# Decoder layer on one core: quadrant sums of the weights added by GpSimd in two parts of 512 columns instead of by VectorE

## The chip, the cores and the metric

The kernel runs on one core of a Trainium2 chip. The metric is the device time of one execution in microseconds, the median of several runs. The engines are called by their names in the profile: PE (TensorE, the matrix engine; PEld is its weight load), DVE (VectorE), ACT (ScalarE), POOL (GpSimd) and SP (SyncE, which here only issues DMAs). Each engine runs its own instructions in the order in which they were put down, and semaphores hold an instruction until what it reads is there.

## The reference

One decoder layer on 512 tokens of width 2048: a normed and modulated input h, a wide projection, two branches (sliding-window attention, and a gated delta rule in 32 heads of 128), a gated merge and an output projection. Cut to what matters here:

```python
proj = h @ w_in
...
o = gated_delta_rule(dq, dk, dv, g, beta)
o = rms_norm(o, dn_norm_w) * jax.nn.silu(dz)
y_b = o.reshape(B, T, DN_VAL) @ w_o_dn
y = jax.nn.sigmoid(mg_a) * y_a + jax.nn.sigmoid(mg_b) * y_b
return x + gate * (y @ w_out)
```

The change concerns w_o_dn and w_out, the weights of two of these products, before they are used.

## The kernel before, in words

All products are made in float32 out of three matmuls on split operands: a weight tile `raw` is split into `whi` (ScalarE, L61) and `wlo` (VectorE, L62), and L255 to L257 multiply `whi` with both parts of the input and `wlo` with the high part. `channel_tile` (L266) makes one 128x512 tile of the projection with 16 such triples and calls `pump` after every second one. `pump` (L90) lets all other work of the stage go a step further: weight loads and splits that are due, generators with a delay counted in pumps (`go`), and generators with a budget per pump (`paced`, L81): such a generator yields a cost, and goes on when the budgets of enough pumps have summed up to it.

In the stage `delta_heads` (L639) sixteen pairs of heads are worked through, g = 0 to 15, with five channel tiles each (query, two values, two gates; L791). Beside the tiles of one pair run the steps of the pair before:

- `queries` (L821): SyncE loads the decay rows `E` of both heads (L726) and kT (L829); GpSimd masks `E` in place (affine select, L731); ScalarE turns it into exponentials (L737, four per head); GpSimd multiplies the loaded rows `qe` (L848) with the query (L869); a few small products `py`, `pu` follow on PE (L881 to L888), with a copy `Y` (L883).
- `scan` (L902): four chunks of the recurrence, with PE, ScalarE and VectorE in turn. Then the root chain on VectorE: `ms` (L964), a reciprocal square root in ten short operations of 128x8 (L68, and three times L71 to L73), and the scaling of the output `osb` (L971, twice). PE transposes `osb` into `pto` (L296), and VectorE multiplies it by the gate (L978).
- Values go through a convolution on VectorE (`yv`, L593 three times, L600) and are transposed by PE (`ptv`) and copied by ScalarE (`vt`, L818).
- In the first part of the stage VectorE also works off a triangular solve (L766, L774, at the end L784).

The later products with w_o_dn and w_out follow Strassen's scheme with seven products of half-size matrices (`PRODUCTS`, L34). Four of the seven weight factors are sums of weight quadrants. `weight_sums` (L1170) makes them while the heads run: it is started at g = 4 (L658) with a budget of 1.75 per pump, and for each of 24 sets it loads four quadrant pieces of 128x1024 into the tiles q00, q10, q11 and q01 (L1182, one buffer each, 512 KB), yields 10, and then four times adds two pieces in place (L1186), yields 4, stores the sum to DRAM (L1188, `g_d` or `f_d`) and yields 2. The next set's loads go into the same four tiles, so each waits until the store of the old sum has landed. All these DMAs stand in SyncE's one queue, with the loads of raw weights, `qe`, `E`, `kT` and the rest.

`behind` (L259) gives an instruction a dependency without a semaphore on the last matmul issued: it sets where the instruction is put into its engine's order, and holds nothing when the program runs. The order within each engine comes from a scheduler that places instructions by priorities and estimated durations; so another engine or duration can change the places of others.

Of the kernel before, what the change touches and what calls it, by code (L numbers as in the profile page):

```python
# [11 lines left out]
ALU = mybir.AluOpType  # L12
# [5 lines left out]
T = 512  # L18
# [27 lines left out]
class Layer:  # L46
# [1123 lines left out]
    def weight_sums(self, wk):  # L1170

        nc, a = self.nc, self.a
        sets = [(a["w_od"][0], self.g_d[0]), (a["w_od"][1], self.g_d[1]), (a["w_out"], self.f_d)]
        for w, dst in sets:
            for n in range(2):
                for i in range(2):
                    for h in range(2):
                        cols = slice(h * 1024, (h + 1) * 1024)
                        q = []
                        for c, r in ((0, 0), (1, 0), (1, 1), (0, 1)):  # L1180
                            t = wk.tile([P, 1024], F32, tag=f"q{c}{r}", name=f"q{c}{r}", bufs=1)
                            nc.sync.dma_start(out=t, in_=w[2 * c + n, 2 * r + i][:, cols])  # L1182
                            q.append(t)
                        yield 10.0
                        for f, (x, y) in enumerate(((0, 1), (1, 2), (0, 2), (2, 3))):
                            self.behind(nc.vector.tensor_tensor(out=q[f], in0=q[x], in1=q[y], op=ALU.add))  # L1186
                            yield 4.0
                            self.behind(nc.sync.dma_start(out=dst[n, f, i][:, cols], in_=q[f]))  # L1188
                            yield 2.0

# [508 lines left out]
```

## Time and profile before

| | us |
|---|---|
| runs | 2904.66, 2897.58, 2900.23 |
| median | 2900.23 |
| profiled execution, its own time | 2904.38 |
| its span, first to last instruction | 2902.6 |
| busy PE / DVE / ACT / POOL | 2831.1 / 1964.7 / 1187.8 / 138.7 |
| first and last addition L1186 (start) | 1347.9 / 2135.3 |

All times in the traces are microseconds from the span's start. A matmul's busy time overlaps that of the next, so PE's idle time, not its busy time, tells what is lost. In a row of groups, "x96 | 118.6, 1235 | 0.1" reads: 96 instructions, 118.6 us busy in total, 1235 ns mean, 0.1 us of idle time of the engine just ahead of them. In a row of waits stand who waited, for whom, the total in us, how often and the longest. In a row of one line's instructions stand the shortest, median and longest in ns.

### The profile page before, as it was taken

What the parts mean: (1) busy time and instruction counts of PE and PEld (TensorE: products, weight loads), DVE (VectorE), ACT (ScalarE), POOL (GpSimd) and SP (SyncE); (2) the same over time, 40 slices, a digit from 0 to 9 for tenths busy, and PEclk for the clock granted to TensorE, in tenths of its full rate; (3) what the DMA queues carried; (4) which work ended last, traced back from release to release, by engine and by line L of the source; (5) the groups of instructions that cost most, each with busy time, mean ns of one, the idle gap of its engine ahead of it and who ended that gap; (6) DMA issues with size and microseconds to landing.
All of it is one profiled execution on the core that took longest, in us unless ns stands there. A gap on an engine that the chain in (4) does not pass through costs nothing.

```text
span 2902.6 us, 38619 instructions
## 1 busy us (share of the span) xinstructions
PE 2831.1 (98%) x14396; PEld 2322.2 (80%) x14396; DVE 1964.7 (68%) x3173; ACT 1187.8 (41%) x2381; POOL 138.7 (5%) x124
## 2 busy tenths in 40 slices
PE   6899999999999999999999999999999999999999
PEld 5588888877787888888888888878888788878887
DVE  5776686878768766777766666666656766764666
ACT  3356453334454343433433333333334444433343
POOL 0001000000001000010100000000000000000000
PEclk8999999999999999999999999999999999999999
DMA  9877774322243243434787777777746887885784
GB/s 331 325 237 228 242 249 153 112 92 83 96 140 99 95 153 130 134 117 165 253 262 244 232 251 248 241 227 248 246 149 219 283 301 266 294 276 176 244 319 165
DMA packets 229790, 604.28 MB, mean 208 GB/s; under 512 B 78145, under 2 KB 104257, under 8 KB 189153
## 3 DMA queue, kind: packets, MB, share of 16 engines
q1 hardware_dynamic: 229602, 601.81, 62.2%
q8 instruction: 113, 1.85, 0.3%
q14 instruction: 75, 0.61, 0.1%
HBM read 481.32 MB, written 118.18 MB: 207 GB/s over the span
## 4 chain that ended last, share of the span: by engine, by line
PE 85%; DVE 6%; DMA 6%; ACT 2%; issue 1%; POOL 0%; SPq 0%; DVEq 0%; POOLq 0%; ACTq 0%
PE mm L255 20%; PE mm L257 19%; PE mm L256 19%; PE m L256 5%; PE m L255 5%; PE m L257 5%; DMA E<-g_rows 1%; DVE wlo L62 1%; DVE wa L430 1%; PE S L1377 1%; PE O L1428 1%; PE pv L922 1%; PE po L941 1%; DMA g_d<-q 1%; PE pP L296 1%
## 5 line engine op out<-in xcount | busy, mean ns | idle before, releaser
L255 PE MATMUL mm<-hh,whi 128*128 128x512 f32 x2784 | 1131.7, 407 | 2.8 <-ACT mth L285 2.8
L257 PE MATMUL mm<-hh,wlo 128*128 128x512 f32 x2784 | 1091.0, 392 | 0.0
L256 PE MATMUL mm<-hl,whi 128*128 128x512 f32 x2784 | 1088.7, 391 | 0.0
L62 DVE TENSOR_TENSOR wlo<-raw,whi 128x1024 fp32r<-128x1024 f32 (+1 forms) x532 | 655.1, 1232 | 468.3 <-ACT whi L61 456.1
L61 ACT CAST whi<-raw 128x1024 fp32r<-128x1024 f32 (+1 forms) x532 | 555.3, 1045 | 875.1 <-PE mm L256 630.3
L255 PEld LDWEIGHTS mm<-hh,whi 128*128 128x128 f32 x2784 | 524.7, 188 | 114.1 <-issue 9.2
L257 PEld LDWEIGHTS mm<-hh,wlo 128*128 128x128 f32 x2784 | 523.6, 188 | 114.0 <-issue 0.5
L256 PEld LDWEIGHTS mm<-hl,whi 128*128 128x128 f32 x2784 | 525.0, 189 | 100.5 <-issue 1.4
L737 ACT ACTIVATE E<-E,neg_g 128x128 f32<-128x128 f32 x256 | 81.9, 392 | 109.4 <-POOL E L731 106.0
L1186 DVE TENSOR_TENSOR q<-q,q 128x1024 f32<-128x1024 f32 x96 | 118.6, 1235 | 0.1
L774 DVE TENSOR_TENSOR A<-A,atmp 128x62 f32<-128x62 f32 (+30 forms) x124 | 108.3, 873 | 0.5
L766 DVE TENSOR_TENSOR atmp<-A 128x62 f32<-128x62 f32 (+30 forms) x124 | 107.7, 868 | 0.5
L869 POOL TENSOR_TENSOR qe<-qe,yq 128x512 f32<-128x512 f32 x32 | 51.0, 1611 | 939.1 <-DMA qe<-eg_rows 693.5
L942 ACT COPY osb<-po 128x256 f32<-128x256 f32 x64 | 23.8, 372 | 153.0 <-PE po L941 153.0
L731 POOL TENSOR_SCALAR_AFFINE_SELECT E<-E 128x512 f32<-128x512 f32 x64 | 55.0, 869 | 459.9 <-DMA E<-g_rows 381.6
L924 ACT COPY vn<-pv 128x256 f32<-128x256 f32 x64 | 23.8, 372 | 120.7 <-PE pv L922 120.7
L1401 ACT ACTIVATE sm<-sm,mx,rs 128x256 f32<-128x256 f32 (+1 forms) x128 | 71.7, 562 | 3.5 <-DVE mx L1396 3.5
L593 DVE SCALAR_TENSOR_TENSOR yv<-mm,convh,yv 128x511 f32<-128x511 f32 (+2 forms) x96 | 71.3, 743 | 1.0
L929 DVE TENSOR_SCALAR vs<-vn,kd 128x128 f32<-128x128 f32 x96 | 23.1, 284 | 57.6 <-ACT vn L924 57.6
L430 DVE SCALAR_TENSOR_TENSOR wa<-wa,silu_cb 128x2048 f32<-128x2048 f32 x24 | 54.8, 2284 | 6.4 <-DMA silu_cb<-silu_d 6.4
L915 DVE SCALAR_TENSOR_TENSOR r<-pp,neg_eg,vt 128x128 f32<-128x128 f32 x96 | 29.1, 345 | 40.6 <-PE pp L912 40.5
L941 PE MATMUL po<-vn,E 128*128 128x128 f32 x256 | 46.8, 275 | 0.0
(425 smaller groups left out, 3666.1 us busy)
## 6 DMA issues: line engine op xcount, KB each, us to landing
raw<-in_w_ch SPq DMA_DIRECT2D x158, 1024.0 KB
wa<-in_w_ada_ss SPq DMA_DIRECT2D x32, 1024.0 KB
q<-in_w_od SPq DMA_DIRECT2D x64, 512.0 KB
g_d<-q SPq DMA_DIRECT2D x64, 512.0 KB
raw<-g_d SPq DMA_DIRECT2D x32, 1024.0 KB
raw<-in_w_od SPq DMA_DIRECT2D x24, 1024.0 KB
gw<-in_w_ada_gate SPq DMA_DIRECT2D x16, 1024.0 KB
E<-g_rows SPq DMA_DIRECT2D x64, 256.0 KB
```

The costliest lines, as they stand in the source:

```text
L61: self.nc.scalar.copy(out=hi, in_=src)
L62: self.nc.vector.tensor_tensor(out=lo, in0=src, in1=hi.bitcast(F32), op=ALU.subtract)
L255: nc.tensor.matmul(ps, lhsT=wh, rhs=xh, start=first, stop=False)
L256: nc.tensor.matmul(ps, lhsT=wh, rhs=xl, start=False, stop=False)
L257: self.last_mm = nc.tensor.matmul(ps, lhsT=wl, rhs=xh, start=False, stop=last)
L430: nc.vector.scalar_tensor_tensor(out=wa, in0=wa, scalar=1.0, in1=scb, op0=ALU.mult, op1=ALU.mult, accum_out=t[:, j : j + 1])
L737: self.nc.scalar.activation(E[:, c, :], E[:, c, :], AF.Exp, bias=self.neg_g[:, c, h : h + 1])
L766: eng.tensor_tensor(out=t, in0=A[:, m : m + 1, m + 1 :].to_broadcast([P, m, n]), in1=A[:, :m, m : m + 1].to_broadcast([P, m, n]), op=ALU.mult,
L774: self.behind(eng.tensor_tensor(out=A[:, :m, m + 1 :], in0=A[:, :m, m + 1 :], in1=t, op=ALU.add))
L941: nc.tensor.matmul(po[:, e, :], lhsT=M[e][:, c, :], rhs=vn[:, e, :], start=c == 0, stop=True)
L1186: self.behind(nc.vector.tensor_tensor(out=q[f], in0=q[x], in1=q[y], op=ALU.add))
L1401: nc.scalar.activation(t, t, AF.Exp, scale=r[:, h : h + 1], bias=mx[:, h : h + 1], accum_out=den[:, h : h + 1])
```

## The change

Each addition of two 128x1024 pieces goes from VectorE to GpSimd, and is cut into two additions of 512 columns. The yield of 4 behind an addition becomes a yield of 2 behind each half, so that the sum per set is the same, 34. Loads, stores and tiles are as before. From here on the lines behind L1185 have a number one higher: the addition is L1187 in the changed kernel.

```diff
                         yield 10.0
                         for f, (x, y) in enumerate(((0, 1), (1, 2), (0, 2), (2, 3))):
-                            self.behind(nc.vector.tensor_tensor(out=q[f], in0=q[x], in1=q[y], op=ALU.add))
-                            yield 4.0
+                            for k in (slice(0, T), slice(T, 1024)):
+                                self.behind(nc.gpsimd.tensor_tensor(out=q[f][:, k], in0=q[x][:, k], in1=q[y][:, k], op=ALU.add))
+                                yield 2.0
                             self.behind(nc.sync.dma_start(out=dst[n, f, i][:, cols], in_=q[f]))
                             yield 2.0
```

What moves in the engines' orders, at two places. First VectorE, at the root chain of the head pair whose L971 runs at 1924 us in the trace; `q` are the quadrant pieces, `ms`, `roy` and `rot` the root's small tiles, `osb` the output of the scan. Before:

```order
L72 TENSOR_TENSOR rot<-rot,ms 128x8
L1186 TENSOR_TENSOR q_16333<-q_16333,q_16335 128x1024
L73 SCALAR_TENSOR_TENSOR roy<-rot,roy 128x8
L62 TENSOR_TENSOR wlo<-raw,whi 128x1024
L71 SCALAR_TENSOR_TENSOR rot<-roy 128x8
L836 TENSOR_SCALAR epsq<-ss 128x4
L593 SCALAR_TENSOR_TENSOR yv<-mm,convh,yv 128x511
L72 TENSOR_TENSOR rot<-rot,ms 128x8
L593 SCALAR_TENSOR_TENSOR yv<-mm,convh,yv 128x510
L73 SCALAR_TENSOR_TENSOR roy<-rot,roy 128x8
L593 SCALAR_TENSOR_TENSOR yv<-mm,convh,yv 128x509
```

and now, from the last L72 of the same chain through the scaling L971 and a little beyond:

```order
L72 TENSOR_TENSOR rot<-rot,ms 128x8
L73 SCALAR_TENSOR_TENSOR roy<-rot,roy 128x8
L62 TENSOR_TENSOR wlo<-raw,whi 128x1024
L971 TENSOR_TENSOR osb<-osb,roy 128x512 x2
L836 TENSOR_SCALAR epsq<-ss 128x4
L593 SCALAR_TENSOR_TENSOR yv<-mm,convh,yv 128x511
L593 SCALAR_TENSOR_TENSOR yv<-mm,convh,yv 128x510
L593 SCALAR_TENSOR_TENSOR yv<-mm,convh,yv 128x509
L978 TENSOR_TENSOR zh<-pto,zh 128x512
```

Before, the addition and the three convolution steps stood inside the chain; now they stand behind it. Of the twelve root chains between 1347 and 2140 us, three have this stretched form before (one addition and three L593 inside), and none now. On PE four of the transposes' groups `pto` stand one or two triples of matmuls earlier; nothing else is moved by more than one weight split on ScalarE or VectorE.

Second GpSimd, at the same head pair, with the semaphores that each instruction waits for; `qe` are the rows that are multiplied with the query, `E` the decay rows that are masked; DMAHW are semaphores of DMAs, Pool that of GpSimd itself. Before:

```order
L869 TENSOR_TENSOR qe<-qe,yq 128x512 [waits DVE_49,DMAHW3_49,PE_49,Pool_49]
L869 TENSOR_TENSOR qe<-qe,yq 128x512 [waits DMAHW4_49,PE_49,Pool_49]
L731 AFFINE_SELECT E<-E 128x512 [waits DMAHW5_49,Activation_49]
L731 AFFINE_SELECT E<-E 128x512 [waits DMAHW6_49,PE_49,Activation_49]
L869 TENSOR_TENSOR qe<-qe,yq 128x512 [waits DVE_49,DMAHW1_49,PE_49,Pool_49]
```

and now:

```order
L1187 TENSOR_TENSOR q_16401<-q_16401,q_16403 128x512 [waits DMAHW6_49,DMAHW1_49,DMAHW0_49]
L869 TENSOR_TENSOR qe<-qe,yq 128x512 [waits DMAHW3_49,DVE_49,PE_49]
L869 TENSOR_TENSOR qe<-qe,yq 128x512 [waits DMAHW4_49,PE_49]
L1187 TENSOR_TENSOR q_16401<-q_16401,q_16403 128x512
L731 AFFINE_SELECT E<-E 128x512 [waits DMAHW5_49,Activation_49]
L731 AFFINE_SELECT E<-E 128x512 [waits DMAHW6_49,PE_49,Activation_49]
L1187 TENSOR_TENSOR q_16403<-q_16403,q_16405 128x512 [waits DMAHW7_49,Pool_49]
L1187 TENSOR_TENSOR q_16403<-q_16403,q_16405 128x512 [waits Pool_49]
L1187 TENSOR_TENSOR q_16405<-q_16401,q_16405 128x512 [waits DMAHW2_49,Pool_49]
```

One half addition is now in front of the multiplications, one between them and the masks, and the other six of the set behind (three are shown). Over the eleven head pairs with masks behind them, ten half additions stand between L869 and both masks, and two more between the first and the second mask. In the last head pair the two multiplications and the last halves are mixed. The half additions wait for the DMAs that load their pieces (and store the sums before) and for GpSimd's own earlier halves; none of them waits for PE, ACT or DVE.

## The prediction

> **What bounds the kernel now.** I read the page first, then its chain, then the stage of the changed line by windows, then who waits there.
>
> ```profile
> span 2902.6 us, 38619 instructions
> PE 2831.1 (98%) x14396; PEld 2322.2 (80%) x14396; DVE 1964.7 (68%) x3173; ACT 1187.8 (41%) x2381; POOL 138.7 (5%) x124
> PE 85%; DVE 6%; DMA 6%; ACT 2%; issue 1%; POOL 0%; SPq 0%; DVEq 0%; POOLq 0%; ACTq 0%
> L1186 DVE TENSOR_TENSOR q<-q,q x96: 1207/1218/1665, 1347.9 to 2135.3; 128x1024 f32<-128x1024 f32 x96
> ```
>
> TensorE is busy 98% of the span and makes 85% of the chain; DVE, which loses work, is 6% of it. The 96 additions lie between 1347.9 and 2135.3 us. So the first question is what TensorE still loses there (columns: stretch, length, busy time of PE, PEld, DVE, ACT, POOL, granted clock, DMA share, GB/s):
>
> ```profile
> 1340.00:1500.00 160.00, 155.19 (x803) 129.13 (x802) 114.95 (x190) 65.48 (x143) 14.16 (x8) 0.98 0.73 238
> 1500.00:1700.00 200.00, 197.71 (x1051) 164.85 (x1050) 123.07 (x209) 76.52 (x180) 12.96 (x12) 1.00 0.75 247
> 1700.00:1900.00 200.00, 197.42 (x1044) 164.28 (x1043) 126.42 (x210) 76.12 (x183) 16.43 (x12) 1.00 0.75 246
> 1900.00:2140.00 240.00, 235.72 (x1233) 196.30 (x1232) 156.64 (x255) 91.14 (x217) 15.28 (x14) 0.99 0.72 235
> 1452.10:1458.90 6.80, 4.95 (x25) 4.06 (x26) 3.21 (x5) 3.08 (x7) 0.64 (x1) 0.50 1.11 322
> 1926.50:1930.00 3.50, 3.50 (x12) 2.81 (x11) 2.98 (x5) 1.75 (x4) 0.00 (x0) 0.51 0.41 158
> ```
>
> Of 800 us TensorE is idle 4.81 + 2.29 + 2.58 + 4.28 = 14.0 us. Two of its waits are followed by stretches at half clock; with 4.95 and 3.50 us of work in them these cost 2.5 + 1.7 = 4.2 us. So 18.2 us, 0.6% of the time, is all that a perfect cover of this stage could return. What TensorE waits for (waited, times, longest):
>
> ```profile
> PE pto L296 <- DVE osb L971: 5.1, 3, 2.8
> PE py L881 <- DMA raw<-in_w_ch: 3.9, 1, 3.9
> PE ptv L296 <- DVE yv L600: 1.8, 1, 1.8
> PE ptv L296 <- DVE zh L978: 1.7, 1, 1.7
> PE py L881 <- ACT vt L818: 1.3, 2, 0.7
> ACT E L737 <- POOL E L731: 69.7, 14, 9.3
> SPq L1188 <- DVE q L1186: 74.6, 37, 8.1
> ```
>
> The last two are other engines: ScalarE waits 69.7 us for GpSimd's masks, and SyncE 74.6 us for the additions whose stores it issues.
>
> **The change part by part.** It takes 96 x 1235 ns = 118.6 us off DVE and puts 192 half additions on GpSimd. The nearest row is the one GpSimd operation of two SBUF tiles of 128x512 in this stage; the masks, which share its queue, are below it:
>
> ```profile
> L1186 DVE TENSOR_TENSOR q<-q,q 128x1024 f32<-128x1024 f32 x96 | 118.6, 1235 | 0.1
> L869 POOL TENSOR_TENSOR qe<-qe,yq x32: 1260/1506/2380, 1093.4 to 2127.5; 128x512 f32<-128x512 f32 x32
> L731 POOL TENSOR_SCALAR_AFFINE_SELECT E<-E x64: 624/635/4532, 186.4 to 2062.8; 128x512 f32<-128x512 f32 x64
> ```
>
> At the median, 192 x 1.506 = 289 us in 787 us (242 at the shortest, 457 at the longest): GpSimd stays under 60% and bounds nothing by its sum. By order the adds carry waits for loads and for GpSimd itself, none for TensorE, so they run when their loads have landed and not at DVE's place.
>
> *The root chain on DVE: gain.* Where an addition stood inside the chain L964 to L971 (the first pair of rows under the change), DVE's chain was stretched, with three L593 also inside. That is so in three heads of the stage, and "pto <- L971" is waited for exactly 3 times.
>
> ```profile
> 1919.12 0.16 DVE L71 SCALAR_TENSOR_TENSOR rot<-roy 128x8 f32<-128x8 f32 x1
> 1921.50 1.02 DVE L71 SCALAR_TENSOR_TENSOR rot<-roy 128x8 f32<-128x8 f32 x1
> 1922.55 1.18 DVE L72 TENSOR_TENSOR rot<-rot,ms 128x8 f32<-128x8 f32 x1
> 1924.35 1.68 DVE L971 TENSOR_TENSOR osb<-osb,roy 128x512 f32<-128x512 f32 x2
> 1921.21 2.51 POOL L869 TENSOR_TENSOR qe<-qe,yq 128x512 f32<-128x512 f32 x2 [63.37 <-DMA qe<-eg_rows]
> 1923.67 1.22 POOL L731 TENSOR_SCALAR_AFFINE_SELECT E<-E 128x512 f32<-128x512 f32 x2
> ```
>
> This is the largest of the three: the stretched chain ran into GpSimd's two multiplications. Now all chains have the short form, and would end before those. I take the whole row and the half clock behind it: -(5.1 + 1.7) = -6.8 us. By order TensorE also takes four of its pto groups one or two triples of matmuls earlier, which spends part of what the shorter chain gives; and if GpSimd's adds meet the chain none of it comes. The term lies between -6.8 and 0; the rows of the orders decide for the first. Next late is then ptv, whose 1.8 and 1.7 us hang on DVE operations that come after ScalarE's tanh.
>
> *Port contention: small loss.* In those rows a 128x8 operation of 0.16 us took 1.18 beside a GpSimd operation: 1.02 us of holding per GpSimd operation. All 192 adds could hold DVE 196 us, none could hold it 0. DVE without the additions is busy (521.1 - 118.6) / 800 = 50%, so half of them, 98 us, is a fair upper value, less than the 118.6 removed. DVE's load therefore falls, but a held operation is late by 1 us where the addition before it made it late by 1.2. I take +1.5 us on TensorE, between 0 and the third rival below. The Trainium skill (SBUF — State Buffer, Who interferes with whom) says that a DVE instruction with two SBUF inputs and a GpSimd instruction that reads SBUF exclude each other, and that the second is blocked until the first is done. By it the hold would be the whole add, 289 us for 192 and not 196; the trace agrees on who is held, and its holds are about 1.0 of 1.26 us.
>
> *The masks behind the adds: loss.* GpSimd's queue now has adds between the multiplications L869 and the masks L731 (the second pair there). Over the eleven heads with masks, 10 stand ahead of both masks and 2 ahead of the second alone: 12 x 1.506 = 18.1 us (15.1 to 28.6) more of ScalarE's wait for masks, if their inputs are there. Behind that wait ScalarE holds weight casts, PSUM copies and the tanh of TensorE's next work:
>
> ```profile
> 1446.07 4.53 POOL L731 TENSOR_SCALAR_AFFINE_SELECT E<-E 128x512 f32<-128x512 f32 x1 [1.44 <-DMA E<-g_rows]
> 1445.70 4.41 DVE L784 TENSOR_TENSOR A<-A,bet 128x4096 f32<-128x4096 f32 x1
> 1450.64 1.28 ACT L737 ACTIVATE E<-E,neg_g 128x128 f32<-128x128 f32 x4 [9.25 <-POOL E L731]
> ```
>
> Here a DVE operation held the mask, ScalarE stood 9.25 us, and TensorE's longest wait (py, 3.9 us) followed; so short waits are covered and long ones are not. On the average 8.9 us of TensorE's idle (14.0 - 5.1) stand against 69.7 us of this wait, 13%; at the margin it can be all. I take 40%, between them but nearer to the average, since the mean wait is 69.7 / 14 = 5.0 us and the covered ones are of that size: +7.2 us. The adds themselves wait for the loads of their quadrants, and a late load would hold the qe and the masks queued behind; SyncE issues most of those loads ahead of E's, so I cost this at nothing beyond the 28.6. Against this, the removed additions no longer hold the masks: two masks took 3.20 us in one head where the median makes 1.27.
>
> ```profile
> 1722.08 3.20 POOL L731 TENSOR_SCALAR_AFFINE_SELECT E<-E 128x512 f32<-128x512 f32 x2
> 1723.13 1.65 DVE L1186 TENSOR_TENSOR q<-q,q 128x1024 f32<-128x1024 f32 x1
> ```
>
> About 1 of those 1.9 us is the addition's; I take three such heads, at the same 40%: -1.2 us.
>
> *SyncE: small gain.* The store of a sum is ahead of loads of qe and E, which the masks need. One such link is on the chain in order of time:
>
> ```profile
> 1569.62 1.23 DVE q L1186
> 1570.87 7.39 DMA g_d<-q
> 1579.65 5.56 DMA E<-g_rows
> 1587.16 2.15 ACT E L737 x7
> ```
>
> With adds that run as soon as loads land, SyncE's 74.6 us mostly go; it then waits for the landing of the store or for TensorE instead. Were GpSimd late, each store would be later by up to one add. Between -4 and +4; I take -1.0 us.
>
> Sum: -6.8 + 1.5 + 7.2 - 1.2 - 1.0 = -0.3 us, from 2904.4 (span 2902.6 and 1.8 around it) to 2904.1. The profiled execution lies 4.2 us above the median of 2900.2; on the median the forecast is 2900 us: no change that shows (0.3%, 8.7 us, is about what this kernel's measurement can tell).
>
> **The rivals.** *DVE's relief wins.* The chain's waits go, SyncE runs ahead, masks come earlier, and TensorE keeps 14 of the 18.2 us: 2886 us. For it: the three irregular chains and the three waits match, and 521 us of DVE fall to 402. Against it: 8.9 us of the idle hang on ScalarE and loads.
>
> *The masks come later and ScalarE stops TensorE (slower).* All 18.1 us of the adds reach TensorE, with half clock behind two more waits (4.2 us): 2900 + 18.1 + 4.2 - 6.8 = 2916 us. It decides once an add between L869 and L731 meets a head whose ScalarE wait is already above about 5 us. For it: the 9.25 us case. Against it: that one was 4.5 us from a single operation.
>
> *A run of adds meets the root chain.* GpSimd runs eight adds back to back, and each short operation of the chain loses 1.02 us: 8.2 us in each of 12 heads, 98 us: 2998 us. The skill's rule would give this too. Against it: by order the runs stand after the masks, and the chain ahead of L869; only the last head's qe has adds around it.
>
> That the change does nothing because DVE is off the path is the forecast's own neighbour, 2900 us.
>
> **How the numbers follow.** No change that shows 0.46; DVE's relief 0.29; masks 0.22; runs of adds 0.03. The faster and the no-change case lie side by side, so the range covers both: it goes from the relief's 2886 to just under the masks' 2916, 2914; the runs and the outer parts of both cases are the 2 in 10 left out. Faster 0.29, same 0.46, slower 0.25.
>
> **What would show it.** Right: GpSimd some 430 us busy and DVE near 1.85 ms; "pto <- L971" gone from TensorE's waits; ScalarE's wait for L731 up by 10 to 18 us; TensorE's idle of the stage 10 to 18 us. Wrong: L71 to L73 at 1 us in many heads with pto waiting behind them; or ScalarE's wait for masks smaller than before; or adds far from 1.5 us.

## The result, and the profile after

The changed kernel takes 2933.6 us (median of 4 runs, 2927.4 to 2936.3) against 2900.2 us before: 1.0114 times, 95% interval 1.0102 to 1.0127. It is 33.4 us slower, where 2900 us was forecast. The profiled execution took 2927.35 us.

From the page of the changed kernel, the span, the busy times and the chain:

```profile
span 2925.6 us, 38733 instructions
PE 2836.7 (97%) x14396; PEld 2324.9 (79%) x14396; DVE 1913.6 (65%) x3077; ACT 1186.8 (41%) x2381; POOL 422.8 (14%) x316
PE 82%; DMA 7%; DVE 6%; ACT 2%; issue 1%; SPq 1%; POOL 1%; DVEq 0%; POOLq 0%; ACTq 0%
```

GpSimd is as busy as forecast. VectorE is not: without its additions it should stand at 1964.7 - 118.6 = 1846.1 us, and it stands at 1913.6. The operations left on it took 67.5 us longer. The stage by windows (columns as in the prediction):

```profile
1340.00:1500.00 160.00, 148.30 (x748) 122.36 (x746) 100.38 (x157) 61.97 (x132) 55.44 (x37) 0.96 0.71 228
1500.00:1700.00 200.00, 194.12 (x1021) 161.23 (x1022) 106.73 (x184) 74.69 (x177) 75.73 (x58) 0.99 0.74 240
1700.00:1900.00 200.00, 195.29 (x1033) 161.83 (x1032) 110.86 (x185) 74.41 (x181) 85.53 (x61) 1.00 0.72 235
1900.00:2140.00 240.00, 232.98 (x1210) 193.51 (x1209) 131.94 (x209) 89.73 (x210) 96.83 (x69) 0.99 0.74 237
```

TensorE is idle 11.7 + 5.9 + 4.7 + 7.0 = 29.3 us here, against 14.0 before. What TensorE waits for in the stage (here 1340 to 2200 us), and the two waits of ScalarE and SyncE that the prediction named:

```profile
PE pd L937 <- DVE vs L929: 13.8, 5, 5.4
PE ptv L296 <- DVE zh L978: 9.3, 6, 3.4
PE py L881 <- DMA g_d<-q: 3.2, 2, 1.9
PE py L881 <- ACT vt L818: 2.9, 1, 2.9
ACT E L737 <- POOL E L731: 68.3, 12, 8.6
SPq L1189 <- POOL q L1187: 59.6, 23, 7.7
```

"pto <- L971" is gone, as forecast. ScalarE's wait for masks is where it was (69.7 before). New is pd, which waits for the scaling of `vn` by `kd` into `vs` (L929), and ptv's wait for L978 has grown from 1.7 to 9.3 us. Two more waits, 1.6 us of ptv for L600 and 2.4 us of pu, lie ahead of 1340 us, since the additions now begin at 1305 us. L929 before the change (shortest/median/longest in ns):

```profile
L929 DVE TENSOR_SCALAR vs<-vn,kd x96: 278/284/290, 1127.5 to 2177.1; 128x128 f32<-128x128 f32 x96
```

and after it, with GpSimd's additions, the root's L73 and the convolution steps:

```profile
L929 DVE TENSOR_SCALAR vs<-vn,kd x96: 272/284/1331, 1125.0 to 2205.5; 128x128 f32<-128x128 f32 x96
L1187 POOL TENSOR_TENSOR q<-q,q x192: 1254/1292/2346, 1305.2 to 2164.8; 128x512 f32<-128x512 f32 x192
L73 DVE SCALAR_TENSOR_TENSOR roy<-rot,roy x36: 166/166/170, 1371.4 to 2154.1; 128x8 f32<-128x8 f32 x36
L593 DVE SCALAR_TENSOR_TENSOR yv<-mm,convh,yv x96: 729/743/751, 1098.1 to 2170.5; 128x511 f32<-128x511 f32 x32, 128x510 f32<-128x510 f32 x32, 128x509 f32<-128x509 f32 x32
```

L929, never above 290 ns before, reaches 1331. The root's L73 isn't held at all, nor is L593, which takes one of its two tiles from PSUM. Two places of the timeline show holds at work (start, length, engine, what; x is a count, in brackets the wait ahead). First GpSimd, VectorE and TensorE around 1420 us:

```profile
1417.59 10.12 POOL L1187 TENSOR_TENSOR q<-q,q 128x512 f32<-128x512 f32 x7
1419.42 1.80 DVE L62 TENSOR_TENSOR wlo<-raw,whi 128x1024 fp32r<-128x1024 f32 x1 [1.64 <-ACT whi L61]
1421.14 1.77 DVE L807 SCALAR_TENSOR_TENSOR zh<-zth,zh 128x512 f32<-128x512 f32 x1
1422.84 2.50 DVE L929 TENSOR_SCALAR vs<-vn,kd 128x128 f32<-128x128 f32 x2
1425.40 1.13 PE L937 MATMUL pd<-vs,k 128*128 128x256 f32 x2 [2.32 <-DVE vs L929]
```

Seven additions run back to back. L62 takes 1.80 us where its median is 1.23, L807 1.77 where it is 0.69, two L929 2.50 where they are 0.57: 0.6 + 1.1 + 1.9 = 3.6 us, of which pd waits 2.3. I read it as turns: an addition, a VectorE operation, the next addition, so that each of these operations is longer by up to most of an addition. Then ptv, around 1953 us:

```profile
1950.38 9.88 POOL L1187 TENSOR_TENSOR q<-q,q 128x512 f32<-128x512 f32 x6
1952.99 2.25 DVE L62 TENSOR_TENSOR wlo<-raw,whi 128x1024 fp32r<-128x1024 f32 x1 [4.79 <-ACT whi L61]
1955.16 1.75 DVE L600 SCALAR_TENSOR_TENSOR yv<-th,yv 128x512 f32<-128x512 f32 x1
1956.83 0.68 DVE L978 TENSOR_TENSOR zh<-pto,zh 128x512 f32<-128x512 f32 x1
1957.56 0.74 PE L296 MATMUL ptv<-ident,yv 128*128 128x128 f32 x4 [3.40 <-DVE zh L978]
```

L978 has a tile in PSUM and isn't held itself, but it stands behind two operations that are, late by 1.0 and 1.1 us.

### The profile page after: what moved, and what is told of

Same layout as the page of the kernel before. It is cut to its first block, busy times and chain, and to the rows that moved or that the text cites. A ratio compares the mean times of both kernels' runs of the same rounds, so it can differ in the third digit from the quotient of the medians.

```text
span 2925.6 us, 38733 instructions
## 1 busy us (share of the span) xinstructions
PE 2836.7 (97%) x14396; PEld 2324.9 (79%) x14396; DVE 1913.6 (65%) x3077; ACT 1186.8 (41%) x2381; POOL 422.8 (14%) x316
## 4 chain that ended last, share of the span: by engine, by line
PE 82%; DMA 7%; DVE 6%; ACT 2%; issue 1%; SPq 1%; POOL 1%; DVEq 0%; POOLq 0%; ACTq 0%
PE mm L255 19%; PE mm L256 18%; PE mm L257 18%; PE m L256 5%; PE m L255 5%; PE m L257 5%; DMA g_d<-q 2%; DMA E<-g_rows 1%; DVE wlo L62 1%; DVE wa L430 1%; ACT whi L61 1%; PE S L1378 1%; DMA tt<-ts_d 1%; PE O L1429 1%; PE po L941 1%
## 5 line engine op out<-in xcount | busy, mean ns | idle before, releaser
L62 DVE TENSOR_TENSOR wlo<-raw,whi 128x1024 fp32r<-128x1024 f32 (+1 forms) x532 | 674.8, 1269 | 506.8 <-ACT whi L61 495.9
L1187 POOL TENSOR_TENSOR q<-q,q 128x512 f32<-128x512 f32 x192 | 289.7, 1539 | 186.1 <-DMA q<-in_w_out 75.9
L869 POOL TENSOR_TENSOR qe<-qe,yq 128x512 f32<-128x512 f32 x32 | 49.2, 1552 | 515.6 <-DMA qe<-eg_rows 306.6
L731 POOL TENSOR_SCALAR_AFFINE_SELECT E<-E 128x512 f32<-128x512 f32 x64 | 51.8, 823 | 450.8 <-DMA E<-g_rows 405.3
L774 DVE TENSOR_TENSOR A<-A,atmp 128x62 f32<-128x62 f32 (+30 forms) x124 | 111.9, 902 | 0.4
L929 DVE TENSOR_SCALAR vs<-vn,kd 128x128 f32<-128x128 f32 x96 | 37.6, 433 | 69.2 <-ACT vn L924 69.2
L1234 POOL TENSOR_TENSOR aq<-aq,cos 128x512 f32<-128x512 f32 x16 | 27.0, 1690 | 338.5 <-DMA partner<-aq 318.4
L593 DVE SCALAR_TENSOR_TENSOR yv<-mm,convh,yv 128x511 f32<-128x511 f32 (+2 forms) x96 | 71.2, 742 | 1.5
```

What stands on the lines that cost most here:

```text
L62: self.nc.vector.tensor_tensor(out=lo, in0=src, in1=hi.bitcast(F32), op=ALU.subtract)
L593: nc.vector.scalar_tensor_tensor(out=y[:, s:], in0=ps[:, : T - s], scalar=w[:, j : j + 1], in1=y[:, s:], op0=ALU.mult, op1=ALU.add)
L774: self.behind(eng.tensor_tensor(out=A[:, :m, m + 1 :], in0=A[:, :m, m + 1 :], in1=t, op=ALU.add))
L1187: self.behind(nc.gpsimd.tensor_tensor(out=q[f][:, k], in0=q[x][:, k], in1=q[y][:, k], op=ALU.add))
```

## The experiments

Theory A: what GpSimd reads holds VectorE's operations with two SBUF tiles, and L929, so that TensorE's pd, ptv and pto come late. Theory B: the additions delay the masks behind them in GpSimd's queue, and so ScalarE. Theory D: the order that the scheduler now makes is worse, whoever adds. The held time in the table is worked out from each trace: over all VectorE operations between 1300 and 2180 us, what each took above the median of its kind in the kernel without additions, where that is over 0.15 us. The kernels are in the order of their times; each ratio is to the runs of the kernel before that were made beside it (medians 2898.5 to 2900.9 us).

| kernel | us | ratio, 95% interval | held time, us |
|---|---|---|---|
| long fills | 2892.7 | 0.9974 (0.9963 to 0.9984) | 15 |
| no additions | 2893.8 | 0.9975 (0.9960 to 0.9989) | 9 |
| fills | 2894.9 | 0.9979 (0.9969 to 0.9989) | 13 |
| halves on VectorE | 2897.3 | 0.9983 (0.9973 to 0.9993) | 21 |
| copies | 2898.7 | 0.9996 (0.9983 to 1.0009) | 25 |
| before | 2900.2 | 1 | 19 |
| quarters, L929 on ScalarE | 2907.2 | 1.0024 (1.0014 to 1.0034) | 45 |
| quarters | 2909.8 | 1.0026 (1.0016 to 1.0037) | 56 |
| right halves' sets only | 2910.0 | 1.0043 (1.0029 to 1.0058) | 45 |
| L929 on ScalarE | 2915.1 | 1.0054 (1.0036 to 1.0072) | 64 |
| paced by a semaphore | 2923.6 | 1.0074 (1.0059 to 1.0089) | 64 |
| left halves' sets only | 2924.0 | 1.0081 (1.0062 to 1.0100) | 58 |
| last two of four only | 2925.6 | 1.0088 (1.0065 to 1.0111) | 61 |
| after | 2933.6 | 1.0114 (1.0102 to 1.0127) | 78 |
| eighths | 2938.4 | 1.0139 (1.0092 to 1.0187) | 54 |

**No additions.**

```diff
-for k in (slice(0, T), slice(T, 1024)):
-    self.behind(nc.gpsimd.tensor_tensor(out=q[f][:, k], in0=q[x][:, k], in1=q[y][:, k], op=ALU.add))
-    yield 2.0
+yield 4.0
```

> Leaves out the sums of the quadrants: the pieces are stored as loaded, all loads and stores stay, no engine adds anything. It is the floor of what moving the additions off VectorE could give. Theory A (GpSimd's additions hold VectorE's operations, several in a row, and TensorE's pd and ptv come late): the time falls below the kernel before, 2880 to 2893 us, since VectorE loses 118.6 us of additions and nothing is held; L929 has no excess over its 284 ns median, TensorE's wait for L929 (13.8 us after) and for L978 (9.3 us) go below 3 us each. Theory B (the additions hold GpSimd's own masks and so ScalarE): the same floor. Theory D (the order of the instructions that the scheduler now makes is worse by itself, whatever runs on GpSimd): 2925 to 2935 us, and pd still waits for L929.

Measured 2893.8 us, 0.8 us above the range of theories A and B and far from D's 2925. TensorE's two largest waits (that for L978 was expected below 3 us), and a window over the stage and its edges:

```profile
PE py L881 <- ACT vt L818: 4.5, 3, 2.9
PE ptv L296 <- DVE zh L978: 3.6, 5, 2.3
1300.00:2240.00 940.00, 930.45 (x4859) 774.70 (x4858) 495.95 (x935) 368.15 (x846) 52.03 (x50) 1.00 0.72 230
```

pd waits no more. So taking the additions off VectorE is worth 2900.9 - 2893.8 = 7.1 us (by the interval 3 to 12; 2900.9 us is the kernel before beside it), and having them on GpSimd costs 2933.6 - 2893.8 = 39.8 us. The same window of the changed kernel shows the size of it:

```profile
1300.00:2240.00 940.00, 904.75 (x4700) 749.62 (x4699) 538.07 (x877) 350.79 (x813) 345.94 (x242) 0.99 0.68 221
```

TensorE is idle 35.3 us instead of 9.6, which is 25.7 us more. Six stretches at a granted clock of 0.50 come with its stalls, with 21.7 us of work in them, against two with 6.8 us; at half the clock half of that is lost, 10.9 - 3.4 = 7.5 us more. The two make 33.2 us of the 35.5 us between the spans.

**Fills, and long fills: GpSimd's queue without its reading.**

```diff
-self.behind(nc.gpsimd.tensor_tensor(out=q[f][:, k], in0=q[x][:, k], in1=q[y][:, k], op=ALU.add))
+self.behind(nc.gpsimd.memset(q[f][:, k], 0.0))
```

and for the long fills `q[f]`, the whole piece, in place of `q[f][:, k]`.

> Leaves out the sums: in each half addition's place GpSimd fills the same 128x512 half with zeros, so that it writes and reads nothing; queue, order and stores are those of the changed kernel. A fill of this size takes 526 ns in the trace, so GpSimd is busy 101 us with them instead of 290. Theory A in the form that VectorE is held by GpSimd's reading of two tiles: L929's excess is below 2 us, and the time is that of the kernel without additions, within 5 us. In the form that any GpSimd operation holds VectorE: each hold is about 0.5 us, and about 15 us of the 33 us stay. Theory B: the masks wait for fewer microseconds in the queue, so about a third of the loss stays (101 / 290), 2890 to 2905 us, with ScalarE's wait for L731 below 68 us. Theory D: 2925 to 2935 us.

> Leaves out the sums: each half addition becomes a fill of the whole 128x1024 piece with zeros by GpSimd, so that GpSimd's queue is occupied nearly as long as by the additions (twice 0.53 us each, some 200 us), while it reads nothing. Theory A (what GpSimd reads holds VectorE): L62, L600, L807 and L971 are not held, only the scalings L929 a little (2.5 us with the half fills), and the time is 2894 to 2900 us. Theory B (the queue delays masks and multiplications): two thirds of the loss of 39.8 us over the kernel without additions stay, 2915 to 2930 us, and ScalarE's wait for L731 rises above 77 us.

Both take the time of no additions (the long fills lie 1.3 us below theory A's range). With long fills GpSimd spends 181 us (192 of 955 ns on the average) in the additions' places, and ScalarE's wait for the masks is even longer than after the change, where it is 72.8 us in the same window:

```profile
ACT E L737 <- POOL E L731: 75.9, 15, 10.8
1922.92 5.77 POOL L1187 MEMSET q<- 128x1024 f32 x6
1924.96 1.23 DVE L62 TENSOR_TENSOR wlo<-raw,whi 128x1024 fp32r<-128x1024 f32 x1 [8.66 <-ACT whi L61]
1926.10 0.68 DVE L600 SCALAR_TENSOR_TENSOR yv<-th,yv 128x512 f32<-128x512 f32 x1
L929 DVE TENSOR_SCALAR vs<-vn,kd x96: 277/282/1117, 1124.3 to 2171.5; 128x128 f32<-128x128 f32 x96
```

It is the same place as the second timeline above: beside six fills L62 and L600 take their medians, where beside six additions each was late by 1 us. Theory B falls. Two lines are held by fills too, and both are TENSOR_SCALAR: L929, though only for 2.8 us in all, and `epsq` (L836, median 0.16 us), which took 2.15 us twice beside long fills and 3.14 once beside the half fills, against 1.25 at most without additions; each time the L593 right behind it ended with it. The Trainium skill (SBUF — State Buffer, Who interferes with whom) says that a VectorE instruction with two SBUF inputs contends with a GpSimd instruction that reads SBUF and not with one that only writes it, and that tensor_scalar can use a mode that takes both ports; the rows agree on both counts.

**Copies: one input.**

```diff
-self.behind(nc.gpsimd.tensor_tensor(out=q[f][:, k], in0=q[x][:, k], in1=q[y][:, k], op=ALU.add))
+self.behind(nc.gpsimd.tensor_copy(out=q[f][:, k], in_=q[x][:, k]))
```

> Leaves out the sums: each half addition becomes a copy of one 128x512 half by GpSimd, which reads one tile and writes one, between the fill (reads none) and the addition (reads two). The trace has no such copy; by the fill's 0.53 us and the addition's 1.29 us it should take between these. Theory A in the form that any reading by GpSimd holds VectorE: L62 and L929 have excesses of about the copy's share of the addition's (half to all of 21.7 and 14.5 us), and the time is 2905 to 2930 us. In the form that only two inputs hold: as the fill, 2894.9 us within 4 us. The Trainium skill (SBUF — State Buffer, Who interferes with whom) speaks for the first form: it names a GpSimd instruction that reads SBUF, not how many inputs it has. Theory D: 2925 to 2935 us.

2898.7 us: by time the form in which only two inputs hold (within 4 us of the fills). But the trace shows holds:

```profile
L1187 POOL COPY q<-q x192: 600/614/2218, 1302.7 to 2127.3; 128x512 f32<-128x512 f32 x192
L62 DVE TENSOR_TENSOR wlo<-raw,whi x129: 1206/1226/1976, 1308.6 to 2179.9; 128x1024 fp32r<-128x1024 f32 x129
```

A typical hold of L600 is 0.41 us, against 1.06 with additions, and L62's excess is 6.7 us instead of 21.7. So reading one tile holds as well, below what the expectation took; with a time some 5 us above that without additions, TensorE's slack covers most of these holds.

This kernel also settles theory D. In its trace every instruction of VectorE, ScalarE and GpSimd and every DMA of SyncE stands at the same place as in the changed kernel's, and so do all but 24 of TensorE's 14396 matmuls; these 24 lie within two groups of pu. Only what GpSimd does in the 192 places differs, and 35 us go with it.

**Halves on VectorE: the engine alone.**

```diff
-self.behind(nc.gpsimd.tensor_tensor(out=q[f][:, k], in0=q[x][:, k], in1=q[y][:, k], op=ALU.add))
+self.behind(nc.vector.tensor_tensor(out=q[f][:, k], in0=q[x][:, k], in1=q[y][:, k], op=ALU.add))
```

> The changed kernel with the half additions on VectorE instead of GpSimd: same halves, same order written, 192 additions of about 0.61 us, which put some 118 us back on VectorE. Theory A (what GpSimd reads holds VectorE's operations ahead of pd, ptv and pto): nothing is held, so L929's excess is below 1 us and the time is 2893 to 2903 us, between the kernel without additions (2893.8) and the kernel before (2900.9); VectorE's load is then not what costs. Theory D (the order of the instructions): 2925 to 2935 us. Should the additions' whole presence on VectorE be worth what the prediction's first term said, the halves give back part of its 6.8 us and the time is about 2897 us.

2897.3 us, 36 us below the changed kernel with the same pieces in the same places of the program (they took 0.68 us each and not 0.61). Its order isn't the changed kernel's: 102 of VectorE's 3077 other instructions stand elsewhere. So the copies are the stricter test of theory D; both speak against it. It is also the fastest kernel here that computes the sums, 0.17% (0.07 to 0.27%) below the one before. TensorE waits for

```profile
PE pto L296 <- DVE osb L971: 5.6, 3, 2.0
PE pd L937 <- DVE vs L929: 1.2, 1, 1.2
```

so the root chain still loses what it lost before.

**L929 on ScalarE: pd's share.**

```diff
-nc.vector.tensor_scalar(out=vs[:, e, :], in0=vn[:, e, :], scalar1=self.kd[:, c, 2 * g + e : 2 * g + e + 1],
-                        scalar2=None, op0=ALU.mult)
+nc.scalar.activation(vs[:, e, :], vn[:, e, :], AF.Copy, scale=self.kd[:, c, 2 * g + e : 2 * g + e + 1])
```

> The changed kernel with one more change: the scaling of vn by kd into vs (L929) is done by ScalarE, 96 small activations, so that the operation in front of pd can't be held by GpSimd. It measures that one consumer's share. Theory A: TensorE's wait for L929 (13.8 us) and the half clock behind its stalls go, 10 to 18 us in all, so 2916 to 2924 us; the waits of ptv for L978 stay near 9 us, as its operations are still held. If the loss came as a train in which pd's wait only uncovers another (ptv, py), the time stays above 2925 us.

2915.1 us, 18.6 us better than the changed kernel, 1 us below theory A's range. (L978 is L975 here.)

```profile
PE ptv L296 <- DVE zh L975: 8.1, 6, 2.4
PE pd L934 <- ACT vs L929: 6.0, 2, 5.1
```

Three of pd's five waits are gone, ptv's stay. The one long wait of pd stays too: it comes at 1407 us, where `vn` itself is late. The changed kernel's trace shows the same wait, 5.4 us at 1410 us, and where it comes from:

```profile
1401.99 1.37 DVE L774 TENSOR_TENSOR A<-A,atmp 128x236 f32<-128x236 f32 x1
1407.85 1.91 ACT L779 COPY atmp<-A 64x1024 f32<-64x1024 f32 x1 [8.25 <-DVE A L774]
1409.66 0.36 ACT L924 COPY vn<-pv 128x256 f32<-128x256 f32 x1
```

Beside seven additions six VectorE operations, four of them of the triangular solve, are late by 5.0 us together between 1395 and 1405 us (the L774 shown takes 0.40 us without additions). ScalarE's copy of the solved `A` (L779) waits for them 8.25 us, where it waited 1.9 before the change, and the copy `vn` stands behind it. So this is a hold as well, by way of ScalarE.

**Quarters, and quarters with L929 on ScalarE.**

```diff
-for k in (slice(0, T), slice(T, 1024)):
+for k in (slice(0, 256), slice(256, T), slice(T, 768), slice(768, 1024)):
...
-    yield 2.0
+    yield 1.0
```

> The same sums on GpSimd in four parts of 256 columns instead of two of 512: 384 additions of about half the time, the sum on GpSimd near 290 us or somewhat above. Theory A: a hold is what is left of one addition, so each held operation loses about 0.5 us instead of 1.0, more operations are held, but the trains in front of pd and ptv are shorter; L929's excess falls below 9 us (14.5), and the time lies between, 2908 to 2925 us. Theory B: the queue is as long as before, 2930 to 2940 us, and nothing changes in ScalarE's wait for L731 (68.3 us). Theory D: unchanged within 5 us.

> Both mends together: additions on GpSimd in four parts of 256 columns, and L929 on ScalarE. Theory A with independent consumers: from 2909.8 us the waits of pd (9.0 us) and the half clock behind the longest go, 2896 to 2902 us, no slower than the kernel before. If the waits behind take over (ptv for L978, py), 2904 us or more.

Quarters take 2909.8 us, as theory A had it (L929's excess is 9.4 us, where less than 9 was expected):

```profile
L1187 POOL TENSOR_TENSOR q<-q,q x384: 717/740/2687, 1305.3 to 2149.4; 128x256 f32<-128x256 f32 x192
L807 DVE SCALAR_TENSOR_TENSOR zh<-zth,zh x32: 678/694/1226, 1121.0 to 2175.7; 128x512 f32<-128x512 f32 x32
```

L807's longest is 0.53 us over its median, where it is 1.09 (1779 ns) with halves. Both mends together give 2907.2 us, as the form had it in which the waits behind take over: L929's move brought 2.6 us at most (the ratios 1.0026 and 1.0024 aren't told apart). pd's short waits went (seven waits became one, of 5.3 us), ptv kept 6.5 of its 7.5 us, and py's wait for `vt` rose from 1.8 to 4.7 us.

**Eighths.**

```diff
-for k in (slice(0, T), slice(T, 1024)):
+for k in (slice(p * P, (p + 1) * P) for p in range(8)):
...
-    yield 2.0
+    yield 0.5
```

> The same sums on GpSimd in eight parts of 128 columns. The unblocked addition took 1.254 us at 512 columns and 0.717 at 256, 2.1 ns a column and 0.18 us fixed, so an estimate of 0.45 us each and some 345 us in all for 768. Theory A with the hold as the rest of one addition: each hold is 0.2 to 0.3 us, held time on VectorE falls from 56 us (quarters) to 25 to 45 us, and the time from 2909.8 to 2898 to 2906 us. If held time follows GpSimd's busy time and not the size of a part: 2908 to 2920 us.

2938.4 us (2929.7 to 2960.0): no better than halves (the intervals overlap) and far slower than quarters, and neither form foresaw it. GpSimd is busy with them for 400 us and not 345. Most holds are 0.26 us, as expected, but four L62 are held 3.9 to 7.5 us, one of them here:

```profile
1947.44 9.92 POOL L1187 TENSOR_TENSOR q<-q,q 128x128 f32<-128x128 f32 x24
1949.76 8.69 DVE L62 TENSOR_TENSOR wlo<-raw,whi 128x1024 fp32r<-128x1024 f32 x1 [6.47 <-ACT whi L61]
PE ptv L296 <- DVE zh L978: 13.9, 4, 10.4
```

Through most of 24 short additions back to back VectorE didn't finish one operation, and ptv waited 10.4 us at once. The turns that are seen with halves and quarters don't always come here. What decides it was not tried.

**Paced by a semaphore.**

```diff
-self.behind(nc.gpsimd.tensor_tensor(...))
+self.behind(nc.gpsimd.tensor_tensor(...), kind=mybir.DependencyClass.Sync)
```

(`behind` passes this class on where it had NoSync.)

> The changed kernel with one difference: each half addition waits for the matmul that stands ahead of it in program order, by a semaphore, where the changed kernel only orders them without a wait. So the halves can no longer run back to back. Theory A: an addition now holds one VectorE operation at a time, 1 us, which the slack of pd (about 1.1 us) and ptv mostly covers; L929's excess stays below 14.5 us, runs of three to six additions are gone from the stage, and the time is 2895 to 2915 us. Theory B: the masks in GpSimd's queue now also wait for TensorE through the addition ahead of them, so ScalarE's wait for L731 rises from 68.3 us, and the time is 2935 us or more.

2923.6 us: neither range, though GpSimd now waited 305 us, 78 times, for TensorE. pd has one wait left, but others came:

```profile
PE ptv L296 <- DVE zh L978: 13.7, 6, 4.0
PE py L881 <- ACT vt L818: 7.5, 4, 3.4
PE pto L296 <- DVE osb L971: 4.1, 3, 1.6
L73 DVE SCALAR_TENSOR_TENSOR roy<-rot,roy x37: 166/166/1291, 1299.9 to 2145.5; 128x8 f32<-128x8 f32 x37
```

Runs of four or more additions back to back went from 24 to 2, but the additions met the root chain now, which they had missed before, and pto is back. So the form of theory A in which only trains of additions hurt is wrong: held time fell little (78 to 64 us), and it found other waits.

**Half of the additions, three ways.** First the last two of each four on GpSimd; then the sets of the left halves of the weights' columns; then those of the right halves. The rest is whole on VectorE. The condition is `f < 2`, then `h`, then `not h`.

```diff
+if f < 2:
+    self.behind(nc.vector.tensor_tensor(out=q[f], in0=q[x], in1=q[y], op=ALU.add))
+    yield 4.0
+else:
     for k in (slice(0, T), slice(T, 1024)):
...
```

> Of each set's four additions the first two stay whole on VectorE and the last two are made by GpSimd in halves: 96 halves on GpSimd instead of 192, and runs of at most four. Theory A: the held time on VectorE falls by about half (the sum of excesses of L62, L600, L929, L807 from 60 us to about 30), and the time lies half way between the kernel without GpSimd's additions (about 2894 to 2900 us) and the changed one (2933.6): 2910 to 2920 us. If a threshold decides (only long runs reach TensorE), 2898 to 2908 us. Theory D: no rule for the time; by it the order of this kernel is its own.

> Half of the additions again, but divided by sets: the sets of the left halves of columns wholly on GpSimd in halves, those of the right halves wholly on VectorE, so that GpSimd's runs don't begin at the end of a VectorE addition as in the kernel with the last two of each four (2925.6 us, held time 61 us against 78 with all on GpSimd). If that coupling made half the dose cost nearly the whole: held time near the middle of before and after (19 and 78 us), 45 to 52 us, and 2908 to 2918 us. If half the additions reach nearly the same VectorE operations whatever sets them off, or the additions kept on VectorE are the other part of the cost: 2920 us or more.

> The complement of the kernel with half of the sets on GpSimd: now the sets of the right halves of columns go to GpSimd, those of the left halves to VectorE, again 96 halves on GpSimd. The other half kept the waits of pd (12.1 us) and lost those of ptv for L978. Theory A with a place for each set (the left halves' runs meet the scan, the right halves' runs meet ptv): here pd's wait for L929 falls below 3 us, ptv's for L978 is 5 us or more, and the time is 2904 to 2914 us. If it is not the place but any exposure of VectorE that costs the same: again 2920 to 2928 us, with pd's wait above 8 us.

2925.6, 2924.0 and 2910.0 us. The first misses both its ranges, and the second falls under its second form, 2920 us or more: half of the additions cost most of the whole. The third, as theory A had it, shows that the place decides. TensorE's two largest waits with the left halves' sets on GpSimd, and then with the right:

```profile
PE pd L937 <- DVE vs L929: 12.1, 6, 2.7
PE py L881 <- ACT vt L818: 8.1, 4, 3.4
```

```profile
PE ptv L296 <- DVE zh L978: 15.1, 6, 4.2
PE pd L937 <- DVE vs L929: 2.3, 1, 2.3
```

Each set's run has its place in a head pair: the left ones meet the scan, where L929 makes pd late, the right ones the operations ahead of ptv. Over the kernel before beside each (2899.3 and 2898.5 us) they cost 24.7 and 11.5 us, 36 us together, against 33.4 for all. Why the last two of each four cost 25 us isn't told apart: there GpSimd's additions begin when a VectorE addition ends (342 us of GpSimd's idle time ended so), L62's excess is 24.5 us, higher than with all of them, and pto waits 7.8 us for L971 again.

## Why the prediction was wrong

*The root chain, -6.8 us: right, as far as the runs tell.* The waits of pto are gone and the chain's operations are not held. Without additions TensorE waits 4.5 us at py and 3.6 at ptv, where it was 5.2 and 3.5 before, so pto's 5.1 us is what went. All that VectorE's relief brings is 7.1 us (3 to 12), with the smaller terms (-1.2 and -1.0) in it; these aren't told apart. The first rival's 14 us wasn't there to be had.

*Port contention, +1.5 us: this step failed.* It said that "a held operation is late by 1 us where the addition before it made it late by 1.2", as if the two cancelled. The size of a hold was right (1.06 to 1.08 us with halves), and the held time, 78 us, lay below the 98 us of the bound. What was wrong is that an addition on VectorE has a fixed place in its order and makes one operation late, while the same work on GpSimd comes in runs as its loads land, and makes each VectorE operation with two SBUF tiles, and L929, wait in turn. Long runs aren't needed for the loss, as the paced kernel shows. VectorE's busy time fell by 51 us, yet at the two places shown its operations in front of pd and ptv were 2 to 4 us late. The step priced a sum of holds and not what stands behind them; pd, with little slack, wasn't named. With the half clock that follows a stall, the term measures 39.8 us (2933.6 - 2893.8), as fills in the additions' places cost nothing and the order is excluded.

*The masks behind the additions, +7.2 us: wrong, near 0.* ScalarE's wait for L731 didn't rise (68.3 us), and long fills in the same places cost nothing at 75.9 us. Why the additions ahead of the masks don't lengthen that wait stays open.

*The third rival* had the mechanism, a run of additions that takes 1 us from each operation of a chain, but put it at the root chain, whose place by order it then took as the evidence against. That evidence held (L71 to L73 are not held); the chains ahead of pd and ptv, L62 with L807 and L929, or L62 with L600 and L978, weren't looked at. Hence 0.03 for this mechanism, which then cost 33 us net and not 98. The rule of the Trainium skill that stood beside it (SBUF — State Buffer, Who interferes with whom) spoke against the change, and the runs with additions agree on who is held (L62, L600, L807 by 1.1 us); the L62 of 8.69 us among additions of 0.44 us goes beyond one hold.

*The masks rival's 2916 us* has the sign by another mechanism, which the fills exclude.

## What to carry to other kernels

Before work moves to GpSimd, list the VectorE operations that read two SBUF tiles, and those that a trace shows held as L929 is here, and see which of them stand shortly ahead of a wait of the bounding engine: each can be late by nearly one GpSimd operation, and several in a row by several. VectorE's busy share says nothing of this: here it was 56% busy in the stage, and had no slack at the places that count. A hold also reaches TensorE through ScalarE, as at L779. Cutting the moved work into parts shortens each hold to a point (quarters gained 24 us on halves here, eighths lost 29 on quarters), and leaving it on VectorE in smaller pieces was better than any form on GpSimd that was tried.

## What the runs showed of the hardware

A full hold, seen most clearly at L807, is the shortest addition's time less about 0.18 us: 1.08 us of 1.25 at 512 columns, 0.53 of 0.72 at 256, 0.26 of 0.44 at 128. The additions are late in turn: 192 whose shortest took 1.254 us made GpSimd busy for 289.7 us, 1.51 each. With 24 additions of 128 columns back to back one VectorE operation of 1.23 us took 8.69; beside additions of 512 none of its line took over 2.31. Operations with one of two tiles in PSUM were not held by additions (L593, longest 751 ns, and L978, 684 ns). Fills held TENSOR_SCALAR operations (L929 up to 1117 ns, L836 up to 3139), while L62 and L600 kept their medians beside fills.
